# Low weight parts: which come by accumulating DMA; three branch units ahead; first input stacks on the Pool queue

## The chip, the cores and the metric

The kernel runs on one core of a Trainium2 chip. The metric is the device time of one execution in microseconds (us); smaller is better. The core has five engines with in-order queues of their own: TensorE (PE in the profile), VectorE (DVE), ScalarE (ACT), GpSimd (POOL, here mostly an issuer of DMAs) and SyncE (SP, which only issues DMAs). DMA engines move data beside them.

## What is computed

A two-layer trunk on 272 tokens (16 of them learned) and 1024 channels in float32. Each layer is a half-step SwiGLU block, a token mixer with two parallel branches (a diagonal complex state-space scan and an attention with forget gates), and a second half-step SwiGLU block. Cut to what matters:

```python
def s5_mixer(u, ...):            # u: (1, 272, 512): 32 groups of 16 channels, 64 complex states each
    bu_re = einsum('blgc,gpc->blgp', ug, b_re); bu_im = ...   # input products
    ...                                                       # times coef; a_r, a_i = exp(lam * dt)
    _, _, h_re, h_im = lax.associative_scan(_complex_combine, (a_r, a_i, bb_re, bb_im), axis=1)
    y = einsum('blgp,gcp->blgc', h_re, c_re) - einsum('blgp,gcp->blgc', h_im, c_im) + d_skip * ug
    z = gelu(y) @ w_glu
    return z[..., :512] * sigmoid(z[..., 512:])

for l in range(2):
    h = h + 0.5 * swiglu(rmsnorm(h, g_ffn1[l]), w1_gate[l], w1_up[l], w1_down[l])
    n = rmsnorm(h, g_mix[l])
    z = n @ w_in[l]                       # columns: u, q, k, v, f, gates
    gates = sigmoid(z[..., o_g:] + b_gate[l])
    y_a = s5_mixer(u, ...)                # branch a
    y_b = forgetting_attention(q, k, v, f_logit + b_f[l])     # branch b, 8 heads of 64
    merged = gates[..., :1024] * (y_a @ w_br_a[l]) + gates[..., 1024:] * (y_b @ w_br_b[l])
    h = h + merged @ w_o[l]
    h = h + 0.5 * swiglu(rmsnorm(h, g_ffn2[l]), w2_gate[l], w2_up[l], w2_down[l])
return rmsnorm(h[:, 16:], g_final)
```

## The kernel before

Activations lie transposed: channels on the 128 partitions, tokens along the row, in groups of 128 channels. Weights stream from memory in units of 128 x 1024 float32 (512 KB) and are used in one fixed order. Full precision is kept by splitting: a weight `w` is cast to a high part `wh` (line 169, ScalarE) and a low part `wl = w - wh`, and each product is three matmuls, wh by the high part of the activations, wh by their low part, and wl by the high part (lines 331 to 333). A unit is 24 matmuls, some 3 us.

**Two ways to a low part.** `Weights.high` issues the raw load on SyncE (line 148, four `raw` buffers) and the cast. Where `by_dma(i)` says no, `Weights.low` subtracts on VectorE (line 203). Where it says yes, ScalarE writes `-wh` (line 174) and the Pool queue issues a DMA that reads the same 512 KB again and adds it onto that (line 178). `wh` and `wl` have five buffers each (`LEAD` is 4), so a unit's cast goes ahead once the unit five before it is done.

**The order.** It is written by the program itself. Every unit ends in `tick()`, which casts one unit ahead, runs the functions that `later(n, f)` has put n ticks away, subtracts one low part, and then takes steps of a background generator up to a budget; `ssm_branch` is that generator and feeds VectorE with the scan between the weights' work. Functions in `mids` are issued inside the next unit.

**The mixer's units**, by their number in the layer's mixer (u0 has number 68 in layer 0, so u6 is `wl74`): u0 to u3 the state-space input, u4 the forget gates (narrow), u5 to u8 values, u9 to u12 keys, u13 to u16 queries, u17 to u32 gates, u33 to u44 the branch section, u45 to u52 the output projection. In the branch section stand four units of `branch_b` (attention side), four of the glu (the state-space side's, needs the end of the scan) and four of branch a (line 1215 merges both). `gates(k)` scales gate rows on VectorE and takes their sigmoid on ScalarE (line 1138), k at a time.

**First stacks.** `have_u(m)` scales the product of u-unit m, splits it, and `put(q, x)` copies for each quarter q three pieces of 32 rows (34 KB each, line 797) into one stack of 96 rows: high, low, high. The state product `bu(j)` (line 678), with j = 4m + q, multiplies that stack; its result goes to the one pair of banks that VectorE reads in line 700, so `bu(j+1)` waits until `bu(j)` has been read there. For m = 0 the stacks of q = 0, 1 are issued in one tick and those of q = 2, 3 in the next (`q // 2`).

Of the kernel before, what the change touches and what calls it, by code (L numbers as in the profile page):

```python
# [17 lines left out]
D = 1024  # L18
KD = D // P
# [4 lines left out]
NF = DFF // P  # L24
DEPTH = 2
# [9 lines left out]
QKV_BUDGET = 1800.0  # L35
GATE_BUDGET = 2700.0
LATE_BUDGET = 2600.0
EARLY_B = 2
LATE_GATES = 16
MID = 6  # L40
WARM = 10
START = 8
BLOCK = 1024
LOWS = LEAD + 1
DMA_LOW = (2 * NF + 3 * KD + 1, 2 * NF + 3 * KD + 43)
BROWS = 96
DELAY = 1
STACKS = (0, 1, 4, 7)
# [35 lines left out]
def plan():  # L84
    units = layer_units() * DEPTH
    blocks, where, off = [], [], 0
    for i, w in enumerate(units):
        if i > 4 and blocks and blocks[-1][1] + w <= BLOCK:
            blocks[-1][1] += w
        else:  # L90
            blocks.append([off, w])
        where.append((len(blocks) - 1, blocks[-1][1] - w, w))
        off += w
    return blocks, where, off


BLOCKS, WHERE, NCOL = plan()
# [36 lines left out]
class Weights:  # L134
# [46 lines left out]
    @staticmethod  # L181
    def by_dma(i):

        i %= len(WHERE) // DEPTH
        return DMA_LOW[0] <= i < DMA_LOW[1] and i % 2 == 0 and WHERE[i][2] == D

    def low(self, parts=1):
        i, nc = self.nl, self.nc
# [24 lines left out]
def body(tc, nc, ins, out):  # L213
    v, s, pe = nc.vector, nc.scalar, nc.tensor

    with (
# [15 lines left out]
        def big(n, dt=F32):  # L232
            return Tiles(halves, n, dt)
# [38 lines left out]
        def later(n, fn):  # L272
            queue.append((state["tick"] + n, fn))
# [23 lines left out]
        def tick():  # L297
            state["tick"] += 1
            pump = not state.pop("pumped", False)
            if pump:  # L300
                W.high()
            due(state["tick"])
            if pump:
                W.low()
            background()
            while tails:
                tails.pop(0)()
# [38 lines left out]
        def split(hi, lo, x, then=None, when=None):  # L346
            s.copy(hi, x)

            def low():
                v.tensor_sub(lo, x, hi.bitcast(F32))  # L350
                if then is not None:
                    then()

            if when is None:
                later(1, low)
            else:
                when(low)
# [417 lines left out]
        def mixer(l, hh, hl, t0, finish):  # L775
# [6 lines left out]
            def scaled(ps, dst, lo, by=None):  # L782
                if by is None:
                    v.tensor_mul(dst[:, lo:], ps[:, : T - lo], rstd[:, lo:])
                else:
                    v.scalar_tensor_tensor(dst[:, lo:], ps[:, : T - lo], by, rstd[:, lo:], ALU.mult, ALU.mult)
                banks.give(ps)
# [3 lines left out]
            def have_u(ps, m):  # L791

                scaled(ps, yr(m), 0)

                def put(q, x):
                    for i, part in enumerate((uh, ul, uh)):
                        nc.sync.dma_start(
                            x(q)[32 * i : 32 * i + 32].bitcast(F32), part(m)[32 * q : 32 * q + 32].bitcast(F32)
                        )
                    later(DELAY, lambda: us.__setitem__(4 * m + q, x))  # L800
                    if q == 3 and m == 3:
                        uh.give()
                        ul.give()

                def done():
                    x = big(4, F32R)
                    first = state["tick"]
                    for q in range(4):
                        at = first + (q // 2 if m == 0 else q) + STACKS[m]
                        queue.append((at, lambda q=q: put(q, x)))  # L810

                split(uh(m), ul(m), yr(m), done)
# [3 lines left out]
            for m in range(4):  # L816
                if m == 0:
                    first = [bank(), bank()]
# [279 lines left out]
            for i in range(16):  # L1098
# [5 lines left out]
                g, m = (gB, i) if i < 8 else (gA, i - 8)  # L1104
# [29 lines left out]
            def gates(k):  # L1134
                for g, o, m in gate_todo[:k]:
                    if (m if o else 8 + m) >= 16 - LATE_GATES:
                        v.tensor_mul(g(m)[:, t0:], g(m)[:, t0:], rstd[:, t0:])
                    s.activation(g(m)[:, t0:], g(m)[:, t0:], AF.Sigmoid, bias=pc("bg", l, o + m))  # L1138
                del gate_todo[:k]

            def branch_b(i):
                hi, lo = W.take()
                for k in range(2):
# [7 lines left out]
                    later(2, e)  # L1151
                gates(2 if i < EARLY_B else 1)
                tick()

            ya = big(8, F32R)
            gelus()
            for i in range(EARLY_B):
                branch_b(i)
# [40 lines left out]
            for i in range(4):  # L1199
                if i + EARLY_B < 4:  # L1200
                    branch_b(i + EARLY_B)
                hi, lo = W.take()
# [23 lines left out]
            first = [bank(), bank()]  # L1226
# [145 lines left out]
def _stream(inp):  # L1372
# [3 lines left out]
    def put(a):  # L1376
        units.append(np.ascontiguousarray(a).reshape(P, -1))
# [10 lines left out]
    def pair(w, c):  # L1388
        t = _tiles(w)
        for a, b in c:  # L1390
            put(np.concatenate([t[a], t[b]], axis=1))

    for l in range(DEPTH):
# [5 lines left out]
        for o in (O_V, O_K, O_Q, O_G + D, O_G + D + 512, O_G, O_G + 512):  # L1399
            for a in _tiles(w[:, o : o + 512]):  # L1400
                put(a)
        for i in range(EARLY_B):
            pair(inp["w_br_b"][l], [(2 * i, 2 * i + 1)])
        pair(inp["w_glu"][l], [(4 + i, i) for i in range(4)])
        for i in range(4):
            if i + EARLY_B < 4:
                pair(inp["w_br_b"][l], [(2 * (i + EARLY_B), 2 * (i + EARLY_B) + 1)])
# [88 lines left out]
```

## Time and profile before

| | |
|---|---|
| median of 3 runs | 1210.58 us (1209.94 to 1210.86) |
| profiled execution | 1211.13 us, span 1209.4 us |
| TensorE busy | 1183.8 us, 98% of the span, 9737 matmuls |
| VectorE busy | 880.7 us, 73% |
| ScalarE busy | 686.1 us, 57% |
| GpSimd busy | 47.1 us, 4% |
| mean granted TensorE clock | 0.996 |

The span is the time from the first to the last instruction of one profiled execution; the execution's time is a little longer. TensorE's busy share is that of pipelined matmuls whose ends are modelled, so what can be lost or won shows in its idle stretches: each row of a timeline names, in brackets, the idle time before an instruction and the instruction or DMA that ended it.

### The profile page before, as it was taken

The page shows a single profiled execution, that of the slowest core. Times are in us where ns is not written, and L with a number is a line of the kernel's source. Part 1 is how long each engine was busy: PE and PEld are TensorE (multiplying, and loading weights), DVE is VectorE, ACT ScalarE, POOL GpSimd, SP SyncE. Part 2 cuts the span into 40 slices and gives each one's busy share as a digit, 9 for nine tenths or more (in the row PEclk, how much of TensorE's full clock was granted, in tenths as well). Part 3 has the DMA queues.
Part 4 walks back from the last instruction along what each step waited for, and adds up shares of the span by engine and source line. Part 5 has one row for each costly group of instructions (what it writes and reads, how often), then busy time and mean ns, then how long its engine had stood idle before and what let it go on. Part 6 is the DMA issues. An engine that isn't in the chain of part 4 may idle for free.

```text
span 1209.4 us, 24167 instructions
## 1 busy us (share of the span) xinstructions
PE 1183.8 (98%) x9737; PEld 1160.3 (96%) x9737; DVE 880.7 (73%) x1676; ACT 686.1 (57%) x1095; POOL 47.1 (4%) x60
## 2 busy tenths in 40 slices
PE   9999999999999999999999999999999999999997
PEld 8999999888899999999999999998988899999997
DVE  7967889788787678997565555657998887666653
ACT  7556445668677575444454444447587865544542
POOL 0000001010000000000000000001100100000000
PEclk9999999999999999999999999999999999999998
DMA  7767556797577677655555665557986665655551
GB/s 239 209 204 232 169 170 180 201 258 195 145 174 190 188 222 209 187 171 172 182 169 177 175 175 178 165 181 197 257 216 158 185 193 166 223 179 189 180 174 66
DMA packets 67840, 226.74 MB, mean 187 GB/s; under 512 B 8688, under 2 KB 12144, under 8 KB 67728
## 3 DMA queue, kind: packets, MB, share of 16 engines
q1 hardware_dynamic: 61088, 202.41, 53.1%
q0 software_dynamic: 6224, 22.17, 10.5%
q8 instruction: 76, 1.25, 0.4%
q10 hardware_dynamic: 416, 0.62, 0.1%
q14 instruction: 36, 0.29, 0.1%
HBM read 220.77 MB, written 1.05 MB: 183 GB/s over the span
## 4 chain that ended last, share of the span: by engine, by line
PE 83%; issue 5%; DMA 4%; DVE 3%; ACT 3%; POOL 0%; SPq 0%; POOLq 0%; ACTq 0%; DVEq 0%
PE ps L333 26%; PE ps L331 26%; PE ps L332 26%; DMA raw<-wts 2%; DMA wl<-wts 1%; ACT wh L169 1%; PE ps L690 1%; PE ps L1011 1%; DVE wl L203 1%; DMA m<-m 1%; DVE m L700 1%; DVE p L700 1%; ACT m L1138 0%; DVE g L766 0%; PE bu L678 0%
## 5 line engine op out<-in xcount | busy, mean ns | idle before, releaser
L331 PE MATMUL ps<-m,wh 128*128 128x272 f32 (+1 forms) x2944 | 850.2, 289 | 4.9 <-DVE t L1186 3.8
L333 PE MATMUL ps<-m,wl 128*128 128x272 f32 (+1 forms) x2944 | 846.2, 287 | 2.9 <-DMA wl<-wts 2.5
L332 PE MATMUL ps<-m,wh 128*128 128x272 f32 (+1 forms) x2944 | 843.3, 286 | 0.4
L169 ACT CAST wh<-raw 128x1024 fp32r<-128x1024 f32 (+2 forms) x378 | 387.4, 1027 | 395.9 <-issue 204.7
L331 PEld LDWEIGHTS ps<-m,wh 128*128 128x128 f32 x2944 | 555.6, 189 | 10.8 <-DVE t L1186 4.6
L333 PEld LDWEIGHTS ps<-m,wl 128*128 128x128 f32 x2944 | 555.5, 189 | 4.2 <-DMA wl<-wts 3.4
L332 PEld LDWEIGHTS ps<-m,wh 128*128 128x128 f32 x2944 | 555.5, 189 | 1.6 <-DVE m L350 0.9
L203 DVE TENSOR_TENSOR wl<-raw,wh 128x1024 fp32r<-128x1024 f32 (+2 forms) x338 | 399.4, 1185 | 7.1 <-ACT wh L169 5.8
L424 DVE TENSOR_TENSOR t<-t,ps 128x272 f32<-128x272 f32 (+1 forms) x88 | 38.0, 432 | 77.6 <-PE ps L333 71.9
L452 DVE TENSOR_TENSOR t<-ps,rstd 128x272 f32<-128x272 f32 (+1 forms) x32 | 14.0, 437 | 84.7 <-PE ps L333 84.7
L418 DVE TENSOR_TENSOR t<-ps,rstd 128x272 f32<-128x272 f32 (+1 forms) x88 | 38.2, 434 | 43.9 <-PE ps L333 43.1
L178 POOL DMA_DIRECT2D wl<-wts x40 | 34.8, 869 | 737.4 <-ACT wl L174 553.2
L700 DVE TENSOR_TENSOR p<-bu,E 128x544 f32<-128x544 f32 x64 | 43.7, 720 | 12.1 <-PE bu L678 10.2
L429 DVE TENSOR_TENSOR m<-t,m 128x272 fp32r<-128x272 f32 (+1 forms) x88 | 37.9, 431 | 14.5 <-ACT m L426 14.3
L700 DVE TENSOR_TENSOR m<-g,E 128x544 f32<-128x544 f32 x64 | 45.7, 717 | 0.0
L426 ACT CAST m<-t 128x272 fp32r<-128x272 f32 (+1 forms) x88 | 36.2, 411 | 14.9 <-DVE t L424 14.6
L766 DVE TENSOR_TENSOR_SCAN g<-ssm_mag,p 128x272 f32<-128x272 f32 x64 | 43.4, 711 | 0.9
L174 ACT ACTIVATE wl<-wh 128x1024 fp32r<-128x1024 f32 x40 | 42.4, 1061 | 1.3
L419 ACT ACTIVATE t<-t 128x272 f32<-128x272 f32 (+1 forms) x88 | 37.2, 423 | 8.5 <-DVE t L418 8.2
L364 ACT ACTIVATE m<-h,par 128x272 fp32r<-128x272 f32 (+1 forms) x48 | 24.5, 518 | 12.6 <-DVE h L454 7.4
L367 DVE SCALAR_TENSOR_TENSOR m<-h,par,m 128x272 fp32r<-128x272 f32 (+1 forms) x48 | 23.3, 493 | 8.6 <-ACT m L364 8.5
L389 DVE RECIPROCAL rstd<-t 128x272 f32<-128x272 f32 (+1 forms) x6 | 11.0, 1837 | 19.7 <-ACT t L388 19.7
(230 smaller groups left out, 684.6 us busy)
## 6 DMA issues: line engine op xcount, KB each, us to landing
raw<-wts SPq DMA_DIRECT2D x344, 512.0 KB, 4.1
wl<-wts POOLq DMA_DIRECT2D x40, 512.0 KB, 7.6
raw<-wts SPq DMA_DIRECT2D x32, 384.0 KB, 3.6
m<-m SPq DMA_DIRECT2D x96, 34.0 KB, 5.8
m<-B SPq DMA_DIRECT2D x8, 384.0 KB, 6.2
h<-hT SPq DMA_DIRECT2D x4, 272.0 KB, 5.2
Bs<-B POOLq DMA_DIRECT2D x8, 128.0 KB, 5.0
m<-C SPq DMA_DIRECT2D x2, 512.0 KB, 6.9
```

The source lines that it names most:

```text
L169: nc.scalar.copy(hi[:, c : c + w // parts], r[:, c : c + w // parts])
L174: nc.scalar.activation(lo[:, :w], hi[:, :w].bitcast(F32), AF.Copy, scale=-1.0)
L203: nc.vector.tensor_sub(lo[:, k], r[:, k], hi[:, k].bitcast(F32))
L331: pe.matmul(ps[:width, :n], lhsT=a, rhs=mh, start=first and i == ks[0], stop=False)
L332: pe.matmul(ps[:width, :n], lhsT=a, rhs=ml, start=False, stop=False)
L333: pe.matmul(ps[:width, :n], lhsT=b, rhs=mh, start=False, stop=last and i == ks[-1])
L418: v.tensor_mul(x[:, :n], pg[:, :n], rstd[:, t0:])
L419: s.activation(y[:, :n], x[:, :n], AF.Silu)
L424: v.tensor_mul(y[:, :n], y[:, :n], pu[:, :n])
L429: v.tensor_sub(al(f)[:, t0:], y[:, :n], ah(f)[:, t0:].bitcast(F32))
L700: v.tensor_tensor(d[:, :, :, a : a + TS], x[:, :, a : a + TS].unsqueeze(1).to_broadcast([P, 2, 2, TS]), tab.unsqueeze(2).to_broadcast([P, ...
L766: v.tensor_tensor_scan(g[:, r], mg, p[:, r], 0.0, ALU.mult, ALU.add)
```

## The change

Four edits. `by_dma` gets another rule: within the mixer, u6 to u16 in steps of three (6, 9, 12, 15), then u18 to u48 in steps of two; before it was every even number from 2 to 42 but the narrow unit. Both make 20 low parts by DMA in a layer: u2, u8, u10, u14, u16 go to VectorE, u9, u15, u44, u46, u48 to DMA. `EARLY_B` goes from 2 to 3: three units of `branch_b` stand ahead of the point where the scan must be done, with two gates each. The copies of the first stacks (m = 0) issue on GpSimd's queue instead of SyncE's, and all twelve in one tick.

```diff
--- before.py
+++ after.py
@@ -35,14 +35,14 @@
 QKV_BUDGET = 1800.0
 GATE_BUDGET = 2700.0
 LATE_BUDGET = 2600.0
-EARLY_B = 2
+EARLY_B = 3
 LATE_GATES = 16
 MID = 6
 WARM = 10
 START = 8
 BLOCK = 1024
 LOWS = LEAD + 1
-DMA_LOW = (2 * NF + 3 * KD + 1, 2 * NF + 3 * KD + 43)
+MIX, MIX_END = 2 * NF + 3 * KD, 50
 BROWS = 96
 DELAY = 1
 STACKS = (0, 1, 4, 7)
@@ -181,8 +181,8 @@
     @staticmethod
     def by_dma(i):
 
-        i %= len(WHERE) // DEPTH
-        return DMA_LOW[0] <= i < DMA_LOW[1] and i % 2 == 0 and WHERE[i][2] == D
+        i = i % (len(WHERE) // DEPTH) - MIX
+        return 6 <= i < MIX_END and (i % 3 == 0 if i < 17 else i % 2 == 0)
 
     def low(self, parts=1):
         i, nc = self.nl, self.nc
@@ -794,7 +794,7 @@
 
                 def put(q, x):
                     for i, part in enumerate((uh, ul, uh)):
-                        nc.sync.dma_start(
+                        (nc.gpsimd if m == 0 else nc.sync).dma_start(
                             x(q)[32 * i : 32 * i + 32].bitcast(F32), part(m)[32 * q : 32 * q + 32].bitcast(F32)
                         )
                     later(DELAY, lambda: us.__setitem__(4 * m + q, x))
@@ -806,7 +806,7 @@
                     x = big(4, F32R)
                     first = state["tick"]
                     for q in range(4):
-                        at = first + (q // 2 if m == 0 else q) + STACKS[m]
+                        at = first + (0 if m == 0 else q) + STACKS[m]
                         queue.append((at, lambda q=q: put(q, x)))
 
                 split(uh(m), ul(m), yr(m), done)
```

On GpSimd's queue, at the low parts of the mixer's first units (`wl` is a low part, `m9` the stack, `m3` and `m4` the high and low part of u, m = 0), stands before:

```order
L178 DMA wl70_2694<-wts 128x1024
L779 MEMSET m7_31_2743 128x1088
L779 MEMSET m8_32_2744 128x1088
L178 DMA wl74_2843<-wts 128x1024
L178 DMA wl76_2914<-wts 128x1024
L178 DMA wl78_3028<-wts 128x1024
L178 DMA wl80_3119<-wts 128x1024
```

and after:

```order
L178 DMA wl74_2842<-wts 128x1024
L797 DMA m9_33_2881<-m3_27_2738 32x272
L797 DMA m9_33_2881<-m4_28_2739 32x272
L797 DMA m9_33_2881<-m3_27_2738 32x272 x2
L797 DMA m9_33_2881<-m4_28_2739 32x272
L797 DMA m9_33_2881<-m3_27_2738 32x272 x2
L797 DMA m9_33_2881<-m4_28_2739 32x272
L797 DMA m9_33_2881<-m3_27_2738 32x272 x2
L797 DMA m9_33_2881<-m4_28_2739 32x272
L797 DMA m9_33_2881<-m3_27_2738 32x272
L178 DMA wl77_2967<-wts 128x1024
L178 DMA wl80_3117<-wts 128x1024
```

The twelve copies now stand between the low parts of u6 and u9, and those of u2, u8 and u10 have left this queue. On SyncE's queue at the same place (`raw` is a weight unit, `m9` the first stack) stands before:

```order
L148 DMA raw77_2839<-wts 128x1024
L148 DMA raw78_2877<-wts 128x1024
L797 DMA m9_33_2882<-m3_27_2739 32x272
L797 DMA m9_33_2882<-m4_28_2740 32x272
L797 DMA m9_33_2882<-m3_27_2739 32x272 x2
L797 DMA m9_33_2882<-m4_28_2740 32x272
L797 DMA m9_33_2882<-m3_27_2739 32x272
L148 DMA raw79_2910<-wts 128x1024
```

and after (`m10` is the second stack):

```order
L148 DMA raw77_2838<-wts 128x1024
L148 DMA raw78_2876<-wts 128x1024
L148 DMA raw79_2915<-wts 128x1024
L797 DMA m10_34_2883<-m3_27_2738 32x272
L797 DMA m10_34_2883<-m4_28_2739 32x272
L797 DMA m10_34_2883<-m3_27_2738 32x272
L148 DMA raw80_2963<-wts 128x1024
```

The raw load of u11 (`raw79`) follows that of u10 directly, and that of u12 comes three copies later. On VectorE's queue around the first state product (`bu18`; `p15` is what line 700 makes of it, `wl76` to `wl78` the low parts of u8 to u10) stands before:

```order
L844 TENSOR_TENSOR t2_69_2976<-ps2_60_2893,t4_70_2977 32x272
L845 TENSOR_TENSOR t2_69_2976<-t2_69_2976,rstd_101 32x272
L700 TENSOR_TENSOR p15_2932<-bu18_2958,E_107 128x4x136 x2
L754 TENSOR_TENSOR p15_2932<-p15_2932 128x272
L756 TENSOR_TENSOR p15_2932<-p15_2932 128x2x136
L203 TENSOR_TENSOR wl77_3036<-raw77_2839,wh77_2969 128x1024
L766 SCALAR_TENSOR_TENSOR g21_3038<-ssm_mag_102,p15_2932 128x272 x2
L700 TENSOR_TENSOR p22_3041<-bu19_3015,E_107 128x4x136 x2
L700 TENSOR_TENSOR m13_37_3082<-g21_3038,E_107 128x4x136
```

and after:

```order
L844 TENSOR_TENSOR t2_69_2975<-ps2_60_2898,t4_70_2976 32x272
L845 TENSOR_TENSOR t2_69_2975<-t2_69_2975,rstd_101 32x272
L203 TENSOR_TENSOR wl76_2991<-raw76_2808,wh76_2917 128x1024
L700 TENSOR_TENSOR p15_2928<-bu18_2954,E_107 128x4x136 x2
L754 TENSOR_TENSOR p15_2928<-p15_2928 128x272
L756 TENSOR_TENSOR p15_2928<-p15_2928 128x2x136
L766 SCALAR_TENSOR_TENSOR g21_3034<-ssm_mag_102,p15_2928 128x272 x2
L700 TENSOR_TENSOR p22_3037<-bu19_3016,E_107 128x4x136 x2
L203 TENSOR_TENSOR wl78_3078<-raw78_2876,wh78_3027 128x1024
L700 TENSOR_TENSOR m13_37_3080<-g21_3034,E_107 128x4x136
```

The subtraction of u9 has left the place behind the first product's steps, that of u8 stands ahead of them and that of u10 behind the read of the second product. On ScalarE's queue at the end of the branch section (`wh111`, `wh112` are the casts of u43 and u44, line 347 casts results) stands before:

```order
L1138 ACTIVATE m3_52_4141<-m3_52_4141,par_76 128x272 x3
L347 CAST m12_61_4688<-t1_86_4845 128x272
L1183 ACTIVATE t4_87_4858<-ps2_138_4809 128x272
L347 CAST m12_61_4688<-t4_87_4858 128x272
L169 CAST wh111_4896<-raw111_4752 128x1024
L169 CAST wh112_4911<-raw112_4795 128x1024
L347 CAST m0_63_4864<-t2_88_4932 128x272
L347 CAST m0_63_4864<-t3_89_4936 128x272
```

and after:

```order
L347 CAST m12_61_4721<-t1_86_4880 128x272
L1183 ACTIVATE t4_87_4887<-ps0_140_4847 128x272
L347 CAST m12_61_4721<-t4_87_4887 128x272
L169 CAST wh112_4925<-raw112_4790 128x1024
L174 ACTIVATE wl112_4927<-wh112_4925 128x1024
L169 CAST wh113_4945<-raw113_4828 128x1024
L347 CAST m0_63_4893<-t2_88_4964 128x272
L347 CAST m0_63_4893<-t3_89_4968 128x272
```

The cast of u43 has moved ahead of the last results, and a negated copy of u44 (line 174) stands behind its cast.

## Rows read from the trace of the kernel before

**Rows 1.** Waits of TensorE: engine, line, waited for; us in total, times, longest us.

```profile
PE bu L678 <- DMA m<-m: 5.4, 2, 2.7
PE ps L331 <- DVE t L1186: 3.8, 4, 1.4
PE ps L333 <- DMA wl<-wts: 2.5, 4, 1.1
```

**Rows 2.** TensorE timeline, first state products: start, us, instruction, [idle before <-releaser].

```profile
228.45 0.36 PE L678 MATMUL bu<-m,Bs 96*128 96x272 f32 x1 [2.75 <-DMA m<-m]
...
833.66 0.36 PE L678 MATMUL bu<-m,Bs 96*128 96x272 f32 x1 [2.65 <-DMA m<-m]
```

**Rows 3.** Windows: length; busy (x instructions) PE, PEld, DVE, ACT, POOL; PEclk; DMA share; GB/s.

```profile
235.00:245.00 10.00, 8.05 (x66) 7.78 (x66) 9.65 (x18) 3.31 (x7) 0.84 (x1) 1.00 0.95 239
245.00:255.00 10.00, 9.26 (x74) 9.01 (x74) 8.99 (x15) 8.08 (x18) 0.90 (x2) 1.00 0.99 239
834.00:844.00 10.00, 10.00 (x71) 9.97 (x69) 9.50 (x17) 7.12 (x13) 0.87 (x1) 0.83 0.67 161
```

**Rows 4.** TensorE timeline, later stalls of the same stage.

```profile
244.87 0.28 PE L905 MATMUL ps<-ident,P 128*16 128x128 f32 x1 [1.95 <-ACT P L899]
...
252.97 0.39 PE L333 MATMUL ps<-m,wl 128*128 128x272 f32 x1 [0.74 <-DMA wl<-wts]
...
864.00 0.39 PE L333 MATMUL ps<-m,wl 128*128 128x256 f32 x1 [1.09 <-DMA wl<-wts]
```

**Rows 5.** SyncE timeline, issues of the first stacks.

```profile
220.02 4.00 SPq L797 DMA_DIRECT2D m<-m  x6
```

**Rows 6.** Pool timeline, issue of u6's low part.

```profile
218.92 0.87 POOL L178 DMA_DIRECT2D wl<-wts  x1 [9.89 <-ACT m L347]
```

**Rows 7.** Line 178 from 217 to 258 us: issue ns min/median/max; landing.

```profile
L178 POOL DMA_DIRECT2D wl<-wts x6: 860/866/886, 218.9 to 257.2; - x6
...
DMA to landing us min/median/max: 7.6/8.5/9.2
```

**Rows 8.** ScalarE timeline, the late cast.

```profile
241.66 1.05 ACT L169 CAST wh<-raw 128x1024 fp32r<-128x1024 f32 x1 [6.96 <-DMA raw<-wts]
```

**Rows 9.** TensorE timeline, uses that the sums go by.

```profile
239.99 0.28 PE L333 MATMUL ps<-m,wl 128*128 128x272 f32 x1
...
261.40 0.29 PE L678 MATMUL bu<-m,Bs 96*128 96x272 f32 x1
...
386.37 0.29 PE L333 MATMUL ps<-m,wl 128*128 128x272 f32 x1
...
865.98 0.29 PE L678 MATMUL bu<-m,Bs 96*128 96x272 f32 x1
...
985.37 0.28 PE L333 MATMUL ps<-m,wl 128*128 128x256 f32 x1
```

**Rows 10.** Page, section 5: line 203 over the whole run: busy, mean ns, idle before.

```profile
L203 DVE TENSOR_TENSOR wl<-raw,wh 128x1024 fp32r<-128x1024 f32 (+2 forms) x338 | 399.4, 1185 | 7.1 <-ACT wh L169 5.8
```

**Rows 11.** VectorE timeline, steps of the state-space chain.

```profile
228.97 1.36 DVE L700 TENSOR_TENSOR p<-bu,E 128x544 f32<-128x544 f32 x2 [3.02 <-PE bu L678]
...
258.55 1.35 DVE L700 TENSOR_TENSOR p<-bu,E 128x544 f32<-128x544 f32 x2
...
864.11 1.36 DVE L700 TENSOR_TENSOR p<-bu,E 128x544 f32<-128x544 f32 x2
```

**Rows 12.** VectorE and TensorE timelines, end of that chain in layer 0.

```profile
349.71 1.36 DVE L700 TENSOR_TENSOR m<-g,E 128x544 f32<-128x544 f32 x2
...
353.70 0.78 PE L690 MATMUL ps<-m,Cx 128*32 128x272 f32 x11
```

**Rows 13.** ScalarE timeline, last casts of the branch section, both layers.

```profile
375.45 1.99 ACT L169 CAST wh<-raw 128x1024 fp32r<-128x1024 f32 x2
...
974.48 1.99 ACT L169 CAST wh<-raw 128x1024 fp32r<-128x1024 f32 x2
```

**Rows 14.** Line 178 over the whole run, issue to landing.

```profile
DMA to landing us min/median/max: 5.3/7.6/9.4
```

## The prediction

> **What bounds the kernel now.** I read the waits of TensorE first. Its largest entries come from three places: the first state products of each layer's mixer wait for their stacked input copies, four unit starts wait for a VectorE step behind ScalarE's queue (line 1186), and four low parts that come by DMA are late [rows 1]. The other engines matter only where they make TensorE wait. Then I read TensorE's timeline at those places: 2.75 us idle before the first product in layer 0 and 2.65 in layer 1 [rows 2]; in the stretch of the second the granted clock is 0.83 on the mean, that is, part of it runs at 1.2 instead of 2.4 GHz, after the engine had stood idle [rows 3]. Later in layer 0 stand 1.95 us (a transpose that waits for a ScalarE copy) and 0.74 us (the low part of u12), in layer 1 1.09 us (the low part of u14) [rows 4]. The same table says what limits that stage beside TensorE: from 235 to 255 us the DMA engines are busy to 0.95 and 0.99, and VectorE for 9.65 and 8.99 of each 10 us [rows 3]. So both means of making a low part, the accumulating DMA and the VectorE subtraction, are nearly used up there, and the change trades one for the other.
>
> **First stacks on the Pool queue.** Before, six copies issue on SyncE from 220.02 us in 4.00 us, 0.67 us each, and stand in that queue behind the raw loads; the product starts at 228.45 us [rows 2, 5]. After, they stand in the Pool queue behind the accumulating DMA of u6. That one issues at 218.92 us [rows 6]; the six of this stage need 8.5 us to land at the median (7.6 to 9.2) [rows 7], so it lands at about 227.4 us, 1.0 us before the product starts now. Data ahead of the stacks in either queue thus ends at about the same time. Stacks landing 0.5 to 1.0 us behind it give a product at 227.9 to 228.5 us. I take 0 for the stall in both layers (0.6 us either way each), and leave the clock's dip in layer 1 as it is: 10 us at 0.83 cost 1.7 us [rows 3], and they come or go with that idle time.
>
> SyncE loses these 12 issues, so the raw load of u11 follows that of u10 directly instead of six copies later, and that of u12 comes after three instead of fifteen copies. Late raw data explains the 6.96 us in which ScalarE stands before one cast, and with it the 1.95 us of TensorE, since the copy that TensorE wants is queued behind that cast [rows 4, 8]. That stall loses its cause, and so does the wait for u12 at 252.97 us.
>
> The Pool queue gains 12 issues between the low parts of u6 and u9. One costs between SyncE's 0.67 us and the 0.87 us that Pool takes for a low part [rows 5, 6]: 8.0 to 10.4 us. They begin at about 219.9, and part of them waits until u6's transfer has given back its completion slot at about 227.4; then five more issues follow (3.3 to 4.4 us), and u9's transfer issues at 230.7 to 231.8 us. It lands 7.6 to 9.2 us later [rows 7], at 238.3 to 241.0, against a first use at 239.99 [rows 9]. I take 0.87 and 7.6 us (the stage's DMA load falls): 239.4, in time. The other end costs 1.0 us.
>
> There is one rule to weigh here. The trace first: all six of Pool's issues between 217 and 258 us take 860 to 886 ns [rows 7], in a stretch where VectorE is busy up to 9.65 of 10 us [rows 3], so no issue was held up. The Trainium skill, page "SBUF — State Buffer", section "SBUF: two separate sides", warns of the opposite for DMAs of the Pool queue: their descriptors are written by GpSimd, which is shut out of a port shared with VectorE during some of its operations, and it quotes about 620 ns alone against 3100 ns beside such an operation. By that ratio the 12 issues would take five times as long, and u9 would be late by far more than 1 us; I give it its weight as the slower rival below, and the trace speaks against it.
>
> **Low parts in the first 17 units.** u2, u8, u10, u14 and u16 go from DMA to VectorE, u9 and u15 the other way: three more subtractions per layer, at 1.18 us on the mean [rows 10], and three fewer accumulating transfers of 512 KB. u2's lies in VectorE's slack before the mixer and u8's in the 3.02 us that VectorE idles before the first product [rows 11]. From there to the sixth product u10, u14 and u16 are added and u9, u15 taken off: +1.2 us. This is the place that decides. The sixth product starts at 261.40 us [rows 9]; it overwrites the bank that VectorE reads until 258.55+1.35 = 259.9 us [rows 11], so there are 1.5 us in hand. Without the stalls of 1.95 and 0.74 us TensorE would be there at 258.7. VectorE needs 1.2 us more, and gets back perhaps 1.0 of the 1.36 us that it idles between 235 and 255 [rows 3], since those gaps are waits for ScalarE and TensorE: ready at 260.1 to 260.2. So the product starts at about 260.3, and of 2.7 us **1.1 us** are gained; if no idle time comes back 0.3, if all VectorE work before it hides 2.7. In layer 1 the product stands at 865.98 us [rows 9], VectorE's read ends at 864.11+1.36 = 865.47 [rows 11]: 0.5 us in hand. TensorE without its stall would come at 864.9, VectorE, with an estimated 0.5 us of idle time given back, is ready at 866.2: **-0.3 us**, with ends at -0.8 and +1.1. Together +0.8 (from -0.5 to +3.8).
>
> **Three branch units ahead.** This moves one unit more ahead of the end of the state-space chain, with two gates beside it. The cover isn't short before: VectorE's last step of that chain ends at 349.71+1.36 = 351.1 us, and the products that read it start at 353.70 [rows 12]: 2.6 us to spare, which hold the subtractions that are left over too. If VectorE came out 3.7 us later for its three subtractions, 1.1 us would be short, and the extra unit covers those. I cost the move at nothing for the chain. What it does to the four waits for line 1186 (3.8 us in all [rows 1]) is a shift: ScalarE's queue holds the gates and casts as before, in another order, with two fewer gates in the last of the four glu steps. I take 0.3 us of gain in each layer; the ends are the loss of 1 us and the gain of 1.9 (all of them).
>
> **Low parts of u44, u46, u48.** They go from VectorE, which has room, to DMA. u44's cast starts with the last of the branch section: the two casts there start at 375.45 us and take 1.99, the second at 376.4; in layer 1 at 974.48 and 975.4 [rows 13]. After the start come the cast (1.0 us), the negated copy (same engine and size, taken as equal) and half a us to Pool's issue, 2.5 us in all, then 5.3 to 9.4 us to land, 7.6 at the median [rows 14]: 384.2 to 388.3, median 386.5 in layer 0, and 983.2 to 987.3, median 985.5 in layer 1. The uses are at 386.37 and 985.37 [rows 9]. So the transfer arrives as it is needed: a median wait of 0.1 us, with up to 2 us at the far end. The cast itself may come up to 1 us later behind the moved gates; I take **0.5 us** of loss in each layer. u46 and u48 have the same 10 us from cast to landing, and gain the time that u44 loses.
>
> **Sum.** Stacks 0, first units +0.8, branch order +0.6, late units -1.0: 0.4 us faster than the profiled execution, that is 1210.7 against its own 1211.13. It lies 0.55 us above the median of 1210.58, which makes **1210.2 us**. About 0.2%, 2.4 us, is what a measurement of this kernel can tell from no change.
>
> **Rivals.**
> (1) *The stacks arrive early.* If the copies pass without waiting for u6's transfer, as transfers of 34 KB could, the product starts 2 to 2.75 us sooner in each layer, VectorE's chain with it, and the clock's dip goes: 4 to 5.4 plus up to 1.7 us, about 1204.9. For it: SyncE's raw loads no longer stand in the same queue. Against it: one queue for both, and the transfer ahead ends 1.0 us before today's start. Chance 0.16.
> (2) *VectorE doesn't bind.* Then the first units give 3.8 instead of 0.8: about 1207.2. For it: fewer casts late, so gaps vanish; against it: 9.65 of 10 us busy. Chance 0.12.
> (3) *Slower: the Pool queue runs late.* From the point where u9's transfer issues later than about 232 us, its landing passes 240 and TensorE waits in both layers; with issues of 1.2 us and more for a copy the five behind the slot end 1.6 us later still and u9 costs 2.0 us a layer, and the delay hands u12 its old wait: 4 us. The late units' far end belongs to the same queue: 2 instead of 0.5 us each, 3 us. Either one makes 1213.2 to 1214.2, about 1213.8. For it: three late units in a row with no margin, and 12 issues ahead of u9; against it: issue times that do not vary. Chance 0.24.
> (4) *The change doesn't do what it says*: stacks in the Pool queue land later than today behind more traffic, 0.6 us a layer, and nothing else is gained: 1211.8, inside the same bound. It is part of the forecast's range.
>
> **Chances.** Forecast 0.48, rivals 0.16, 0.12 and 0.24. The forecast's own range is 1208.4 to 1212.4. (1) and (2) reach to 1204.9 and 1207.2, (3) to 1214.2; leaving out 2 in 10 I keep 1206.2 to 1214.0. Faster by over 0.2% (under 1208.2): (1), (2) and nothing else, 0.28. Slower (over 1213.0): 0.24. Same: 0.48.
>
> **What would show it.** Stacks: the idle time before the first product stays near 2.7 us in both layers, and the clock's dip with it; idle time under 1 us proves (1). First units: the waits at the ScalarE copy and for u12 and u14 are gone, and new waits of 1 to 1.5 us stand before the sixth product, for VectorE; none there proves (2). Pool: u9's transfer issues at about 231 us; a wait for a low part at u9 proves (3). Late units: short waits at u44, u46 or u48, under 1 us. Wrong altogether it would be if state products wait for VectorE all through the gates, where I assume room.

## The result

The changed kernel is slower: 1218.2 us at the median (1217.8 to 1221.8, 5 runs) against 1210.9 us for the kernel before beside it (1209.9 to 1213.6, 5 runs). The ratio is 1.0065, with a 95% interval from 1.0054 to 1.0076, or some 8 us (6.5 to 9.2). That lies outside the predicted range of 1206.2 to 1214.0 us, and on the other side of no change than the forecast.

The profiled execution after is the longest of its five, with a span of 1220.0 us. TensorE's waits in it (engine, line, waited for; us in total, times, longest):

```profile
PE bu L678 <- DMA m<-m: 7.3, 2, 3.9
PE ps L333 <- DMA wl<-wts: 6.3, 6, 2.2
PE bu L678 <- issue: 3.9, 2, 2.1
...
PE ps L331 <- DVE t L1186: 1.3, 2, 0.7
```

Against [rows 1], the wait for the first stacks has grown (5.4 to 7.3 us), the late low parts have grown (2.5 to 6.3), those of line 1186 have shrunk (3.8 to 1.3), and one entry is new: state products that wait for nothing the profile names, 3.9 us. TensorE's timeline shows these places (start, us, instruction, [idle before <- what ended it]):

```profile
230.46 0.49 PE L678 MATMUL bu<-m,Bs 96*128 96x272 f32 x2 [3.41 <-DMA m<-m]
...
263.75 0.49 PE L678 MATMUL bu<-m,Bs 96*128 96x272 f32 x2 [1.77 <-issue]
...
390.80 0.39 PE L333 MATMUL ps<-m,wl 128*128 128x272 f32 x1 [1.57 <-DMA wl<-wts]
...
839.41 0.57 PE L678 MATMUL bu<-m,Bs 96*128 96x272 f32 x1 [3.86 <-DMA m<-m]
...
873.95 0.36 PE L678 MATMUL bu<-m,Bs 96*128 96x272 f32 x1 [2.12 <-issue]
...
994.46 0.38 PE L333 MATMUL ps<-m,wl 128*128 128x256 f32 x1 [2.21 <-DMA wl<-wts]
```

The first and the fourth answer to [rows 2], the second and fifth are the sixth state product of each layer ([rows 9], without idle time before), the third and last the low part of u44. The stalls of [rows 4] are gone. Behind two of these waits in layer 0 the granted clock falls (window; length; busy time of PE, PEld, DVE, ACT, POOL; PEclk; DMA share; GB/s):

```profile
230.00:235.00 5.00, 4.54 (x24) 4.58 (x25) 3.49 (x6) 4.33 (x10) 3.06 (x6) 0.66 1.04 263
264.00:268.00 4.00, 4.00 (x24) 4.00 (x24) 3.97 (x8) 1.04 (x1) 0.00 (x0) 0.67 0.97 174
```

A mean of 0.66 is a mixture of the levels 1.2 and 2.4 GHz. TensorE stood idle ahead of both falls.

Where the time goes can be read from the starts of the first low-part matmul of a unit. In this pair of profiles, 10.6 us apart, the stretch from u5 to u17 is longer by 2.5 us in layer 0 and 3.6 in layer 1, that from u33 to u52 by 0.7 and 2.5. Ahead of u5 in layer 0 lie 1.4 us more, in a program that starts alike; the granted clock over the first 100 us is 0.98 instead of 1.00 there. All the rest takes as long as before, to 0.1 us.

On Pool's queue the copies do what the order says. Seven issue behind u6's transfer, the eighth after 5.01 us of waiting for that transfer, then u9's:

```profile
220.21 0.89 POOL L178 DMA_DIRECT2D wl<-wts  x1 [9.99 <-ACT wl L174]
220.78 3.83 POOL L797 DMA_DIRECT2D m<-m  x7
229.62 0.50 POOL L797 DMA_DIRECT2D m<-m  x1 [5.01 <-DMA wl<-wts]
230.43 1.98 POOL L797 DMA_DIRECT2D m<-m  x4 [0.31 <-issue]
232.40 0.97 POOL L178 DMA_DIRECT2D wl<-wts  x1
```

u9's transfer issues at 232.4 us, and no wait at u9 follows, since TensorE came there at 243.5 us instead of 240.0; the transfer landed at 240.6.

### The profile page after: what moved, and what is told of

It reads as the page before. It is cut to its first block, busy times and chain, and to the rows that moved or that the text cites. A ratio compares the mean times of both kernels' runs of the same rounds, so it can differ in the third digit from the quotient of the medians.

```text
span 1220.0 us, 24182 instructions
## 1 busy us (share of the span) xinstructions
PE 1189.9 (98%) x9737; PEld 1167.4 (96%) x9737; DVE 881.6 (72%) x1676; ACT 687.5 (56%) x1095; POOL 59.1 (5%) x84
## 3 DMA queue, kind: packets, MB, share of 16 engines
HBM read 220.77 MB, written 1.05 MB: 182 GB/s over the span
## 4 chain that ended last, share of the span: by engine, by line
PE 87%; issue 4%; DMA 4%; DVE 2%; ACT 1%; POOL 1%; SPq 0%; DVEq 0%; POOLq 0%; ACTq 0%
PE ps L331 27%; PE ps L333 27%; PE ps L332 27%; DMA wl<-wts 2%; DMA m<-m 1%; PE ps L690 1%; PE bu L678 1%; PE ps L1011 1%; DVE g L766 0%; DMA h<-hT 0%; DVE m L700 0%; POOL wl L178 0%; DVE p L700 0%; DVE wl L203 0%; PE ps L1076 0%
## 5 line engine op out<-in xcount | busy, mean ns | idle before, releaser
L203 DVE TENSOR_TENSOR wl<-raw,wh 128x1024 fp32r<-128x1024 f32 (+2 forms) x338 | 399.7, 1186 | 4.6 <-ACT wh L169 3.4
L700 DVE TENSOR_TENSOR p<-bu,E 128x544 f32<-128x544 f32 x64 | 43.7, 720 | 13.7 <-PE bu L678 11.8
L178 POOL DMA_DIRECT2D wl<-wts x40 | 34.9, 873 | 307.1 <-ACT wl L174 144.1
L426 ACT CAST m<-t 128x272 fp32r<-128x272 f32 (+1 forms) x88 | 36.2, 412 | 15.8 <-DVE t L424 15.6
L779 POOL MEMSET m<- 128x1088 f32 x4 | 4.0, 1009 | 448.2 <-PE ps L333 352.7
```

Source lines behind the costliest of these rows:

```text
L203: nc.vector.tensor_sub(lo[:, k], r[:, k], hi[:, k].bitcast(F32))
L700: v.tensor_tensor(d[:, :, :, a : a + TS], x[:, :, a : a + TS].unsqueeze(1).to_broadcast([P, 2, 2, TS]), tab.unsqueeze(2).to_broadcast([P, ...
```

## The experiments

Two theories were on record ahead of each run, A and B. For the first five: A, several places each give a part, chiefly VectorE ahead of the sixth product and the late transfers of the branch section; B, one part makes it all. Later runs have theories of their own. Twelve kernels were run. Ratios are against the kernel before on the same chip.

### One part of the change at a time

**Stacks alone.**

```diff
-                        nc.sync.dma_start(
+                        (nc.gpsimd if m == 0 else nc.sync).dma_start(
...
-                        at = first + (q // 2 if m == 0 else q) + STACKS[m]
+                        at = first + (0 if m == 0 else q) + STACKS[m]
```

> The kernel before with one edit alone: the twelve first stacks issue on the Pool queue, in one tick. Theory A (three places add up): in the changed kernel the first stacks landed right behind u6's transfer, which took 9.1 us instead of 8.5 beside a raw load that now issues earlier; the first state product waited 3.6 us instead of 2.9 in layer 0 and 4.0 instead of 2.8 in layer 1, and the clock fell after both. Alone the edit then costs 2 to 4 us: about 1213 to 1215. Theory B (VectorE's three extra subtractions are the whole loss, and the move of the stacks costs nothing, as forecast): within 1 us of the kernel before.

Measured: 1211.2 us, ratio 1.0004 (0.9995 to 1.0013). The move costs nothing at the median, as B (and the prediction) had it.

**The rule of the first 17 units alone.**

```diff
-        i %= len(WHERE) // DEPTH
-        return DMA_LOW[0] <= i < DMA_LOW[1] and i % 2 == 0 and WHERE[i][2] == D
+        i = i % (len(WHERE) // DEPTH) - (DMA_LOW[0] - 1)
+        return 6 <= i < 43 and (i % 3 == 0 if i < 17 else i % 2 == 0)
```

> The kernel before with one edit alone: the new rule of low parts in the first 17 mixer units, u44, u46 and u48 stay on VectorE, stacks stay on SyncE, two branch units ahead. Theory A: the stalls for late data in the value, key and query units (about 3 us in layer 0, 1.2 in layer 1) go, and a wait for VectorE of 1.5 to 2.3 us stands before the sixth state product, with a clock dip of up to 1.5 us after it: between 1 us faster and 2 us slower than before. Theory B: the whole loss is here, 6 to 8 us slower.

Measured: 1216.2 us, ratio 1.0046 (1.0034 to 1.0058), 5.6 us slower. It is the largest part by far, just under what B gave for it, and far from A's upper end of 2 us. In its profile 4.9 us of the 5.0 lie between u5 and u17 of the two layers. The new wait is there as in the changed kernel:

```profile
PE bu L678 <- DMA m<-m: 7.0, 2, 3.7
PE bu L678 <- issue: 3.9, 2, 2.1
```

**Late units alone.**

```diff
-DMA_LOW = (2 * NF + 3 * KD + 1, 2 * NF + 3 * KD + 43)
+DMA_LOW = (2 * NF + 3 * KD + 1, 2 * NF + 3 * KD + 50)
```

> The kernel before with one edit alone: u44, u46 and u48 also get their low parts by DMA. Theory A: TensorE waits 1 to 1.5 us at u44 in each layer, 2 to 3 us slower in all, about 1213. Theory B: the transfers arrive as they are needed, within 0.5 us of the kernel before.

Measured: 1212.6 us, ratio 1.0013 (1.0004 to 1.0021), 1.6 us slower, between the two. TensorE waits 0.24 us at u44 in layer 0 and 0.51 in layer 1.

**Three branch units ahead alone.**

```diff
-EARLY_B = 2
+EARLY_B = 3
```

> The kernel before with one edit alone: three branch units ahead instead of two. Theory A: ScalarE's queue in the branch section only changes its order: a gain of up to 1 us, or nothing. Theory B: the casts of u38 and u42 come later behind the moved gates, their low parts are late as in the changed kernel (0.3 to 1.5 us each), 1 to 3 us slower.

Measured: 1209.6 us, ratio 0.9991 (0.9983 to 1.0000), 1.1 us faster, which its interval only just tells from nothing, though the late low parts that B named came: 4.2 us of waits for line 178 against 2.5 in [rows 1], in exchange for most of the 3.8 us of line 1186.

The four parts add up to 0.04 + 0.46 + 0.13 - 0.09 = 0.54%, against 0.65% for all together, within the intervals.

### One part taken out of the changed kernel

**Stacks back on SyncE**, the first diff undone.

> The changed kernel, but the first stacks issue on SyncE in two ticks as before. Theory A (the queue makes no difference, since both end behind 512 KB that land at the same time): within 1.5 us of the changed kernel's 1218.2. Theory B (twelve Pool issues ahead of u9 cost on top of the rest): 2 to 4 us faster than the changed kernel.

Measured: 1217.9 us, ratio 1.0062 (1.0050 to 1.0075). No difference to the changed kernel, as A said.

**Late units back on VectorE.**

```diff
-MIX, MIX_END = 2 * NF + 3 * KD, 50
+MIX, MIX_END = 2 * NF + 3 * KD, 43
```

> The changed kernel, but u44, u46 and u48 stay on VectorE. Theory A: the waits at u44 (1.7 and 2.4 us) go and ScalarE loses six negated copies: 3 to 4 us faster than the changed kernel, about 1214.5. Theory B (the wait only moves to the next late unit, since the branch section's ScalarE queue sets it): within 1 us of the changed kernel.

Measured: 1215.8 us, ratio 1.0046 (1.0034 to 1.0059), 2.4 us faster than the changed kernel: less than A's 3 to 4, more than B's 1. The waits at u44 are gone, those at u38 (0.59 and 1.41 us) and at u42 of layer 1 (0.84) stay.

So the loss is some 5.6 us from the first 17 units, as measured alone, and 2.4 us from the late ones, as measured by taking them out; the other two parts come to about a microsecond or less. The rule of the first 17 units and the third branch unit were not taken out of the changed kernel.

### What the first 17 units lose

**u16 stays on DMA.**

```diff
-        return 6 <= i < 43 and (i % 3 == 0 if i < 17 else i % 2 == 0)
+        return 6 <= i < 43 and (i % 3 == 0 if i < 16 else i % 2 == 0)
```

> The rule of the first 17 units alone, as in e2_first17, but u16 stays on DMA: one subtraction fewer on VectorE ahead of the sixth state product, everything ahead of it unchanged. Theory A (VectorE's work up to the sixth product is what e2_first17 lost): the wait before that product falls from 1.9 and 2.3 us to 0.7 and 1.0, the time by 2.4 us, to about 1213.8. Theory B (the stalls and clock dips at the first product are what it lost): no change from e2_first17, 1216.

Measured: 1212.9 us, ratio 1.0014 (1.0004 to 1.0025): one subtraction fewer on VectorE ahead of the sixth product is worth 3.3 us of the 5.6 by the medians, 3.9 by the ratios. The new wait has shrunk by 2.5 us in all, to the numbers expected (0.65 and 1.02 us by starts of matmuls, 0.48 and 0.87 us of idle time); the waits of the first products are about what they were:

```profile
PE bu L678 <- DMA m<-m: 6.5, 2, 3.8
...
PE bu L678 <- issue: 1.4, 2, 0.9
```

What sets the sixth product shows in the time from the second product to it. With the new rule (the changed kernel, e2_first17, a1_sync, a2_nolate) it is 28.4 to 28.5 us in both layers of all four, and in f1_u16dma 27.2 in both: less by one subtraction, 1.22 us long. The stretch in layer 0 of e2_first17, then of f1_u16dma, then of e3_late, which has the old rule here (columns as in [rows 3]):

```profile
235.28:263.70 28.42, 26.67 (x214) 26.37 (x213) 27.37 (x46) 16.73 (x29) 2.58 (x3) 1.00 0.84 219
234.80:261.95 27.15, 26.67 (x214) 26.37 (x213) 26.15 (x45) 17.57 (x30) 2.58 (x3) 1.00 0.82 216
234.96:261.46 26.50, 26.50 (x215) 26.39 (x213) 25.13 (x44) 16.78 (x30) 2.61 (x3) 1.00 0.97 247
```

In the third TensorE is never idle; in the first two it is, and VectorE is busy for all but 1.05 and 1.00 us. The entry "issue" of the wait, which names no engine, is thus a wait for VectorE.

**u9 and u10 change places.**

```diff
-        return 6 <= i < 43 and (i % 3 == 0 if i < 17 else i % 2 == 0)
+        return 6 <= i < 43 and (i in (6, 10, 12, 15) if i < 17 else i % 2 == 0)
```

> The rule of the first 17 units alone, as in e2_first17, but u9 and u10 change places: u9 is subtracted by VectorE, u10 comes by DMA. The count of subtractions ahead of the sixth state product stays. In e2_first17 VectorE stands idle for 1.75 us ahead of the second product's read, where the kernel before subtracts u9. Theory A (it matters where VectorE has room, not only how many subtractions it gets): the wait before the sixth product shrinks by 0.8 to 1.2 us a layer, about 1214. Theory B (only the count matters): as e2_first17, 1216.

Measured: 1213.4 us, ratio 1.0021 (1.0012 to 1.0030), 2.7 us faster than e2_first17 with the same count of subtractions. VectorE's timeline behind the first product, first in e2_first17:

```profile
232.64 1.34 DVE L766 TENSOR_TENSOR_SCAN g<-ssm_mag,p 128x272 f32<-128x272 f32 x2
235.73 1.36 DVE L700 TENSOR_TENSOR p<-bu,E 128x544 f32<-128x544 f32 x2 [1.75 <-PE bu L678]
237.00 1.22 DVE L203 TENSOR_TENSOR wl<-raw,wh 128x1024 fp32r<-128x1024 f32 x1
```

and in f2_swap:

```profile
232.18 1.22 DVE L203 TENSOR_TENSOR wl<-raw,wh 128x1024 fp32r<-128x1024 f32 x1
233.32 1.33 DVE L766 TENSOR_TENSOR_SCAN g<-ssm_mag,p 128x272 f32<-128x272 f32 x2
234.76 1.35 DVE L700 TENSOR_TENSOR p<-bu,E 128x544 f32<-128x544 f32 x2
```

With u9's subtraction in its old place (232.18) VectorE has no gap there; without it, it stands idle until TensorE has made the second product, and does a subtraction right after, where it has no room. The idle time before the sixth product fell from 1.75 to 0.63 us in layer 0, as A has it. In layer 1 of this profile it stayed at 2.1 us:

```profile
261.80 0.36 PE L678 MATMUL bu<-m,Bs 96*128 96x272 f32 x1 [0.63 <-issue]
...
866.97 0.37 PE L678 MATMUL bu<-m,Bs 96*128 96x272 f32 x1 [2.10 <-issue]
```

There the time from the first to the sixth product fell from 871.0 - 836.8 = 34.2 us in e2_first17 to 867.0 - 834.9 = 32.1 us, yet TensorE had lost as much less on the way, so it came as much earlier and waited as long: over the 5 us behind the first product the granted clock is 1.00 in this profile and 0.50 in that of e2_first17. So part of what this layer gained is the clock's, and A's shorter wait was seen in layer 0 alone.

### What the first stacks wait for

**The first three copies on ScalarE's queue.**

```diff
-                        nc.sync.dma_start(
+                        (nc.scalar if m == 0 and q == 0 else nc.sync).dma_start(
```

> The kernel before, but the first three copies of the first stack (those the first state product needs) issue on ScalarE's queue, behind no weight transfer. Theory A (the queue ahead sets the stall): the copies land within 4 us of their issue, the idle time of 2.7 us before the first product and the clock dip shrink to under 1 us in both layers; but the weights' data are not earlier, so most is given back as waits for casts and low parts in the value, key and query units: 1 to 3 us faster. Theory B (the DMA engines are full and every queue lands as late): no change.

Measured: 1211.4 us, ratio 1.0005 (0.9996 to 1.0014): no change, B. On a queue with no weight transfer ahead of them, these 34 KB copies still take 7.2 to 7.7 us to land, little less than those issued beside them on SyncE (8.6 to 9.2). Line 797 on SyncE, then on ScalarE, with the time to landing behind each, and the window in which they land:

```profile
L797 SPq DMA_DIRECT2D m<-m x3: 539/594/595, 220.4 to 221.6; - x3
...
DMA to landing us min/median/max: 8.6/8.9/9.2
...
L797 ACTq DMA_DIRECT2D m<-m x3: 607/716/885, 221.0 to 222.6; - x3
...
DMA to landing us min/median/max: 7.2/7.7/7.7
```

```profile
225.00:230.00 5.00, 1.12 (x10) 0.93 (x8) 1.36 (x4) 3.95 (x6) 0.86 (x1) 0.94 1.04 288
```

### Towards a better kernel

e4_early3 is the one part that gains, and leaves late low parts in the branch section, where VectorE is busy for 5.11 and 6.07 of 10 us before and ScalarE for 9.88 and 9.40 (windows below). So they go to VectorE:

```diff
-EARLY_B = 2
+EARLY_B = 3
...
-        return DMA_LOW[0] <= i < DMA_LOW[1] and i % 2 == 0 and WHERE[i][2] == D
+        rel = i - DMA_LOW[0] + 1
+        return DMA_LOW[0] <= i < DMA_LOW[1] and i % 2 == 0 and WHERE[i][2] == D and rel not in (38, 42)
```

> Three branch units ahead (as in e4_early3), and the low parts of u38 and u42, which come late by DMA there (1.3 and 1.1 us in layer 0, 1.75 at u38 in layer 1), subtracted by VectorE, which is busy for less than 6 of 10 us there; ScalarE loses two negated copies a layer in a stretch where it is busy to 9.9 of 10. Theory A (those transfers set the branch section): 3 to 4 us faster than e4_early3, about 1206. Theory B (ScalarE's order sets it, another wait takes their place): within 1 us of e4_early3's 1209.6.

Measured: 1206.6 us, ratio 0.9965 (0.9951 to 0.9978), 3.0 us faster than e4_early3. With `and rel < 37` for the last condition, u40 goes too:

> As g1_u38u42, and u40 as well on VectorE, so that no low part comes by DMA after u36: one more negated copy off ScalarE's full stretch. Theory A: 0 to 1 us faster than g1_u38u42. Theory B: VectorE fills up, and the branch section waits for subtractions: 1 to 2 us slower than g1_u38u42.

Measured: **1204.0 us**, ratio 0.9944 (0.9929 to 0.9959): 6.2 us faster than the kernel before it ran beside, which no longer leaves the branch section a wait of over 0.5 us. Its windows there:

```profile
357.00:367.00 10.00, 10.00 (x103) 9.56 (x92) 9.03 (x18) 9.84 (x16) 0.00 (x0) 1.00 0.61 193
367.00:377.00 10.00, 10.00 (x82) 10.00 (x81) 8.51 (x18) 7.11 (x15) 0.00 (x0) 1.00 0.52 152
```

and the same in the kernel before:

```profile
357.00:367.00 10.00, 8.66 (x67) 8.23 (x66) 5.11 (x13) 9.88 (x15) 1.69 (x2) 1.00 0.76 186
367.00:377.00 10.00, 9.51 (x71) 8.87 (x71) 6.07 (x14) 9.40 (x19) 0.91 (x2) 1.00 0.96 247
```

TensorE is never idle, VectorE takes up 2.4 to 3.9 us more, and ScalarE has 7.11 instead of 9.40 us in the second. Last, u6 on VectorE as well (`and rel < 37 and rel != 6`):

> As g2_u38tou42, and u6's low part on VectorE, whose subtraction falls in the stretch in which VectorE stands idle ahead of the first state product; the accumulating transfer of u6, which fills the DMA engines while the first stacks wait, is gone. Theory A (that transfer is what the stacks wait for): the wait before the first product falls from about 3.2 to under 1.5 us in both layers, the clock dips go, and 3 to 5 us are gained on g2_u38tou42, about 1200. Theory B (the raw loads alone keep the stacks late, or the time is given back as late casts in the key units): within 1.5 us of g2_u38tou42's 1204.0.

Measured: 1206.1 us, ratio 0.9962 (0.9947 to 0.9976), 2 us slower than g2_u38tou42; not A, and a little worse than B. The stacks wait in the queue now, because the raw load ahead of them needs the buffer that u6's subtraction frees later (SyncE's timeline; before, they issue at 220.02 [rows 5]):

```profile
220.20 2.55 SPq L148 DMA_DIRECT2D raw<-wts  x2
222.84 3.77 SPq L798 DMA_DIRECT2D m<-m  x6
```

## Where the prediction failed

The step that failed is the term of +0.8 us for the first 17 units. Measured alone they cost 5.6 us. Both of its halves were wrong: the stalls counted as gained came back as a longer first wait and a slower clock, and the price of VectorE's work ahead of the sixth product was too low. None of the rivals had this cause: (3), the slower one, put the loss into the Pool queue.

**The stalls went, and the time came back elsewhere.** The sum of the first 17 units began with 2.7 us in layer 0 and 1.1 in layer 1 that the change would free, namely the stalls of [rows 4]. They are gone after it; but in layer 0 the stalls at u12 and at the ScalarE copy are just as gone in e3_late and e4_early3, where the change had touched nothing up to there. The table has the lengths of two stretches (us, from the starts of the first low-part matmul of u5, u14 and u17) and the granted clock over the 5 us behind the first product:

| | u5 to u14, layer 0 | clock | u14 to u17 | u5 to u14, layer 1 | clock | u14 to u17 |
|---|---|---|---|---|---|---|
| before | 35.9 | 1.00 | 11.8 | 35.2 | 0.66 | 11.2 |
| e1_stacks | 33.0 | 1.00 | 12.6 | 36.2 | 0.50 | 11.5 |
| e3_late | 36.2 | 0.50 | 11.8 | 34.5 | 0.66 | 11.5 |
| e4_early3 | 35.8 | 0.50 | 11.8 | 33.9 | 1.00 | 12.3 |
| e5_actq | 36.7 | 0.50 | 11.8 | 34.8 | 0.66 | 11.5 |
| changed kernel | 34.9 | 0.66 | 15.2 | 36.4 | 0.50 | 13.6 |
| e2_first17 | 36.0 | 0.50 | 13.7 | 35.6 | 0.50 | 13.5 |
| f1_u16dma | 35.3 | 0.66 | 12.6 | 33.8 | 0.70 | 12.3 |
| f2_swap | 35.6 | 0.68 | 12.6 | 33.5 | 1.00 | 14.9 |

From u5 to u14 layer 0 takes 35 to 37 us in all of them but one. What differs is where the lost time stands: the profile of before had a shorter wait at the first product, the full clock behind it and late data afterwards; e3_late and e4_early3 have a longer wait with a fall of the clock, and no late data afterwards. TensorE's idle time in e3_late is 3.60 us there, and the clock is 0.52 in the window behind it:

```profile
229.04 0.57 PE L678 MATMUL bu<-m,Bs 96*128 96x272 f32 x1 [3.60 <-DMA m<-m]
```

```profile
230.00:235.00 5.00, 5.00 (x25) 5.00 (x24) 4.41 (x7) 3.25 (x8) 0.86 (x1) 0.52 0.48 116
```

That a TensorE which comes later finds its data there is a reading of these profiles; no run was made for it. The exception is layer 0 of e1_stacks: the first wait is 3.04 us, the clock stays at 1.00, the stalls are gone, and the stretch takes 33.0 us. So the gain can be had where the clock holds, as far as one layer of one profile shows it. u12's raw load issues at 224.9 us there instead of 234.1, earlier as the prediction had it. In the other layer the wait is 4.03 us, the clock 0.50, and the stretch 1.0 us longer than before.

In e2_first17 the account from u5 to u14 against before is, for layer 0 and layer 1: stalls gone, 2.7 and 1.1 us; first waits longer by 0.9 and 0.7; the rest of the stretch, idle time taken off, longer by 1.9 and 0.8, with the clock at 0.50 instead of 1.00 and 0.66. That is a loss of 0.1 and 0.4 us where 3.8 in all were counted as gained. The prediction took 0 for the first wait and left the clock as it was. As the clock behind this wait differs between kernels that do the same up to there, I read one profile's stalls as fixed costs.

**The price of VectorE's subtractions was too low.** The mechanism was named rightly: the sixth product waits for VectorE's read of the fifth. The forecast had a wait of about 1.6 us in layer 0 (260.3 instead of 258.7) and 1.4 in layer 1 (866.3 instead of 864.9); measured by starts of matmuls are 1.9 and 2.3 us. Two steps were wrong. First, I counted one subtraction more and took 1.0 us of VectorE's idle time as given back. From the second product to the sixth there are two more, and VectorE's busy time there is 27.37 us in e2_first17 against 25.13 in e3_late; its idle time in that stretch fell only from 1.37 to 1.05. For u9's subtraction, which the change took away, had stood ahead of the second product, where it filled the wait for it. After the change VectorE is idle there:

```profile
230.98 1.35 DVE L700 TENSOR_TENSOR p<-bu,E 128x544 f32<-128x544 f32 x2 [1.88 <-PE bu L678]
...
235.77 1.36 DVE L700 TENSOR_TENSOR p<-bu,E 128x544 f32<-128x544 f32 x2 [1.23 <-PE bu L678]
237.04 1.22 DVE L203 TENSOR_TENSOR wl<-raw,wh 128x1024 fp32r<-128x1024 f32 x1
```

f2_swap gives that place back and 2.7 us with it, in part by the clock. Second, a new wait ahead of TensorE brought a new fall of the clock in this profile: from 264 to 268 us it is 0.67 on the mean, and 4 us at two thirds cost 1.3 us. No term of the sum had a clock fall at a place that had none before. It does not come each time: e2_first17 and a1_sync have the same wait, and the clock stays at 1.00 behind it in both layers. f1_u16dma takes one subtraction away and 3.3 us with it, 2.5 of them at the sixth product. That VectorE ahead of the sixth product is the main cause is shown by the equal times from the second product to it and by these two runs: from u14 to u17 the two layers of e2_first17 lose 4.3 us of the profile's 5.0. The remainder is the balance of first waits, stalls and clock above, which varies from profile to profile.

**The late units cost 2.4 us instead of 1.0, and the other late waits weren't seen.** The time from u44's cast to its landing was forecast at 10 us and is 390.76 - 380.56 = 10.2. What failed is the start of the cast: it comes right behind the last results of the glu, at 380.56 us, and these come later with a third branch unit ahead of the glu:

```profile
380.23 0.42 ACT L347 CAST m<-t 128x272 fp32r<-128x272 f32 x1 [0.56 <-DVE t L1186]
380.56 1.05 ACT L169 CAST wh<-raw 128x1024 fp32r<-128x1024 f32 x1
381.64 1.06 ACT L174 ACTIVATE wl<-wh 128x1024 fp32r<-128x1024 f32 x1
```

Against [rows 13] (second cast at 376.4) that is 4.1 us, of which about 2.7 are the whole program's lateness at this point (u43's product starts 2.7 us later than before). The remaining 1.5 us stood in the text as an end ("up to 1 us later"), and of the wait that it makes only 0.5 us stood in the sum; measured are 1.57 us at u44 in layer 0 and 2.21 in layer 1. With two units ahead (e3_late) these waits are 0.24 and 0.51 us, and the same transfers cost 1.6 us in all, against the sum's 1.0.

**The stacks: right number, wrong reason.** I took 0, and e1_stacks and a1_sync both measure it. The reason given was that the transfer ahead in either queue ends at the same time. e5_actq has no transfer ahead, and its first product waits no less (3.88 us in layer 0, 3.49 in layer 1); so the queue does not matter. What is left is the DMA engines, busy to 0.9 and more in that window; no run lightened them alone. The nearest is g3_u6, without u6's transfer: its first three copies land 4.1 to 4.9 us after their issue, but issue 2.8 us later. The Trainium skill, page "DMA: Bandwidth & Descriptors", section "Issuing engines are not separate DMA queues", says it: transfers run on the same DMA engines whoever issues them, and another issuer saves only the time of issuing. The trace agrees: 7.2 to 7.7 us to landing from ScalarE's queue, 8.6 to 9.2 from SyncE's.

**Pool late at u9** (the slower rival): it issued at 232.4 us, past the 231 to 232 that I had named, and landed at 240.6 us, after the 240.0 at which it was needed before. That its price did not come was luck: TensorE was 3.5 us later there. Pool's copies take 498 to 854 ns in this stage of layer 0 and the accumulating transfers 867 to 971 ns to issue, so none took the 1.2 us and more of that rival.

**Three branch units ahead**: forecast at +0.6 us, measured +1.1 alone. The cover for the chain's end was not needed: with two units ahead and the added subtractions, e2_first17 takes 38.7 and 37.6 us from u33 to u44 against 38.6 and 38.1 before. What gains, by the waits, is the order of ScalarE's queue (3.8 us for line 1186 become 0.5).

## What to carry to other kernels

When one step is moved between two full engines, ask at which places each has idle time that it can use, and move it only out of full stretches into such gaps; the count of steps alone does not tell (f2_swap and e2_first17 have the same). A stall that follows another in the same stream of data may be the same lateness a second time: compare the length of the whole stretch, and the clock in it, over several profiles before adding stalls up. A transfer takes ten microseconds from its cast to its use here, so a unit whose cast cannot come earlier than that belongs on an engine, as the branch section's units did.

## What was not expected of the hardware

A 34 KB copy on a queue without a weight transfer landed 7.2 to 7.7 us after its issue while the DMA engines were 0.9 to 1.0 busy with 512 KB transfers of other queues: a queue of its own gives a small transfer no precedence here. And what follows the same code varies: the idle time before the first product of layer 0 is 2.75 us in one profile and 3.60 in another of kernels that do not differ up to there, and in the second the clock falls after it and in the first it does not. The length of the wait does not decide it alone: behind waits of 2.75 (before), 3.04 (e1_stacks), 3.21 (e4_early3, layer 1) and 3.46 us (f2_swap, layer 1) the granted clock is 1.00 over the next 5 us, behind 2.65 us (before, layer 1) 0.66 and behind 3.19 us (e4_early3, layer 0) 0.50.
